# Block 1's positions in the order second half, first half, and T4 written over T2

## The chip, the cores and the metric

The kernel runs on one core of a Trainium2 chip. Five engines work side by side, each through its own queue in order: TensorE (PE, matrix products; PEld is its weight load), VectorE (DVE), ScalarE (ACT), GpSimd (POOL) and SyncE (SP, which issues transfers). The metric is the device time of one execution in microseconds; lower is better. The profile comes from one more execution, recorded by the hardware profiler.

## The reference

One encoder layer on x of 1024 positions by 1024 channels, float32: modulation, a Fourier mixing of positions and channels with a linear map, a layer norm, then a gated MLP with a convolution of width 3 over positions, and a last layer norm. The part that the change touches is the MLP's first product:

```python
def conv_gated_ffn(h, w_up, conv_w, conv_b, w_down):
    u = h @ w_up
    up = jnp.pad(u, ((0, 0), (1, 1), (0, 0)))
    u = up[:, :-2] * conv_w[0] + up[:, 1:-1] * conv_w[1] + up[:, 2:] * conv_w[2] + conv_b
    val, gate = u[..., :D_FF], u[..., D_FF:]
    return (jax.nn.gelu(gate, approximate=False) * val) @ w_down
```

D_FF is 2816, so w_up has 5632 columns.

## The kernel before

**Products.** Every float32 product is made of three TensorE products (hl3, L283 to L286): each operand is split into a high part, a float32r rounding made on ScalarE (L53), and a low part, the remainder, made on VectorE or GpSimd (L54); high by high, high by low and low by high are added in PSUM.

**Stages.** First comes the Fourier mixer, then the first norm, which leaves the modulated activations as eight tiles h2t0 to h2t7 (one for 128 channels, 1024 positions each, slots 0 to 7). Then the up-projection, in 22 blocks of 128 value columns and 128 gate columns (j = 0 to 21), and at the end the down-projection.

**Blocks 0 and 1** are multiplied plainly: for value and gate, 8 channel tiles times 3 products over the positions. Block 0 goes through four groups of positions as the activations become ready (their parts are Hh and Hl). Block 1 (L611 to L616) goes through the two halves of positions, ph, 512 each, and in each through v = 0 (value) and v = 1 (gate): four products of 24 matmuls. Its weights' parts, a1, lie in slots 33, 24, 25 and 26.

**Blocks 2 to 21** use Strassen's scheme: the activations are four quarters B (first or second half of channels, kh, by first or second half of positions, ph), and seven products of 12 matmuls replace eight. Four combinations of quarters are needed: T1 = B12 - B11, T2 = B22 - T1, T3 = B22 - B12, T4 = T2 - B21, where the second index is the half of positions. Their raw forms come from comb (L532): T1 and T3 in slots 34 and 35, T2 in 46 and 47, T4 in 31 and 32. t_op (L521) splits T1, T2, T4 into slots of their own; T4's parts go into slots 24, 44, 25 and 26, which hold parts of a0 and a1 until blocks 0 and 1 are multiplied. T3's parts overwrite B12's, that is Hh and Hl of the first four channel tiles, second half of positions (L617 to L619): blocks 2 to 21 don't need B12 itself.

**A block's weights.** Raw halves of block j are two tiles wu (512 KB each); for block 2 in slots 27 and 28, of which 28 first holds u0_0, the value part of block 0 before its convolution. GpSimd makes four sums: S1 and S2 in S12 (slot 31), S3 and S4 in S34 (slot 32); S1 and S4 need the second raw half, S3 only the first (L633 to L636). Seven operands a (A11, S2, S1, A12, S3, S4, A22: products 0 to 6) are split into slots 33, 34, 35, 45, 46, 47 and 48. A block ends in gated (L573): three passes of the convolution for value and gate (L578 on ScalarE, L579 and L580, the taps, on VectorE), GELU (L582), the product, and a write of the result to memory, issued by GpSimd (L588).

**What sets the order.** The program is written block after block, and a list scheduler with a timeline model reorders the instructions of each engine; in this part nothing is ordered by hand. A tile in a slot waits until the last reader of the slot's tile before has finished.

Of the kernel before, what the change touches and what calls it, by code (L numbers as in the profile page):

```python
# [8 lines left out]
F32 = mybir.dt.float32  # L9
F32R = mybir.dt.float32r  # L10
AF = mybir.ActivationFunctionType
ALU = mybir.AluOpType
# [12 lines left out]
ON_POOL = frozenset((  # L25
    "H0", "H1", "T1", "T2", "T4", "a0", "a1", "c1l0", "c1l1", "c1l2", "fb0_0", "fb0_512", "fb1_0", "fe00_512",
    "lb1_512", "lb2_512", "lb3_512", "le00_0", "le10_512", "s0_512", "s2_0", "s3_512", "ve2",
# [9 lines left out]
def encoder_layer(ctx: ExitStack, tc: tile.TileContext, I, out: bass.AP):  # L37
# [8 lines left out]
    def slot(i, shape, dt, name):  # L46
        return big.tile([128] + list(shape), dt, tag=f"s{i}", name=name)
# [4 lines left out]
    def split(hi, lo, src, eng=None):  # L52
        act.activation(hi, src, AF.Copy)  # L53
        (eng or dve).tensor_tensor(lo, src, hi, ALU.subtract)  # L54

    def E(name):
        return pool if name in ON_POOL else dve
# [42 lines left out]
    def xbank(name):  # L100
        n_x[0] += 1
        return bank(n_x[0] % 8, name)
# [326 lines left out]
    for n_t, t in enumerate((1, 2, 0, 3)):  # L429
        ts_ = slice(128 * t, 128 * t + 128)  # L430
        xr = []
        for m, src in ((0, I["x"]), (1, I["xm"])):
            v = slot(25 + (2 * n_t + m) % 3, [D], F32, f"xr{t}_{m}")
# [71 lines left out]
    B = {(kh, ph): [h2t[4 * kh + q][:, 512 * ph : 512 * ph + 512] for q in range(4)] for kh in range(2) for ph in range(2)}  # L505
# [15 lines left out]
    def t_op(name, n, pieces):  # L521
        hi, lo = [], []
        for i in range(2):
            h = slot(T_slots[16 + 4 * n + 2 * i], [2, 512], F32R, f"T{name}h{i}")
            l = slot(T_slots[17 + 4 * n + 2 * i], [2, 512], F32R, f"T{name}l{i}")
            for q in range(2):
                split(h[:, q, :], l[:, q, :], pieces[2 * i + q])
                hi.append(h[:, q, :])
                lo.append(l[:, q, :])
        ops[name] = (hi, lo)  # L530

    def comb(name, x, y, op, sl):  # L532
        out_ = []
        for i in range(2):
            v = slot(sl + i, [2, 512], F32, f"{name}_{i}")
            for q in range(2):
                E(name).tensor_tensor(v[:, q, :], x[2 * i + q], y[2 * i + q], op)
                out_.append(v[:, q, :])
        return out_

    cw = cp.tile([128, NB, 2, 4], F32, name="cw")
# [25 lines left out]
    def plain_mm(acc, w, v, g):  # L567
        for k in range(KT):
            hl3(acc, *w[k, v], g(Hh[k]), g(Hl[k]), k == 0, k == KT - 1)
# [3 lines left out]
    def gated(j, u_v, u_g):  # L573
        tv = []
        for v, u in ((0, u_v), (1, u_g)):
            tt = slot(3 + (2 * j + v) % 3, [S], F32, f"t{j}_{v}")
            w = cw[:, j, v, :]
            act.activation(tt, u, AF.Identity, scale=w[:, 1:2], bias=w[:, 3:4])  # L578
            dve.scalar_tensor_tensor(tt[:, 1:S], u[:, 0 : S - 1], w[:, 0:1], tt[:, 1:S], ALU.mult, ALU.add)  # L579
            dve.scalar_tensor_tensor(tt[:, 0 : S - 1], u[:, 1:S], w[:, 2:3], tt[:, 0 : S - 1], ALU.mult, ALU.add)  # L580
            tv.append(tt)
        act.activation(tv[1], tv[1], AF.Gelu)  # L582
        gg = u_g

        dve.scalar_tensor_tensor(gg[:, 0:512], tv[0][:, 0:512], -1.0, tv[1][:, 0:512], ALU.mult, ALU.mult)
        dve.tensor_tensor(gg[:, 512:513], tv[0][:, 512:513], tv[1][:, 512:513], ALU.mult)
        dve.tensor_tensor(gg[:, 513:1024][:, ::-1], tv[0][:, 513:1024], tv[1][:, 513:1024], ALU.mult)  # L587
        pool.dma_start(gd[j], gg)  # L588
# [3 lines left out]
    for gi, g in enumerate(GRP):  # L592
        for k in range(KT):
            split(g(Hh[k]), g(Hl[k]), g(h2t[k]), E(f"H{gi}") if k % 2 else dve)
        for v in range(2):
# [4 lines left out]
            for k in ((), (), (0, 1), (2, 3), (4, 5), (6, 7), (), ())[2 * gi + v]:  # L600
                ada_mm(G2, l_g2, bk=2, kts=(k,))
    a1 = plain_w(1, (33, 24, 25, 26))
    T1 = comb("T1", B[0, 1], B[0, 0], ALU.subtract, 34)
    T2 = comb("T2", B[1, 1], T1, ALU.subtract, 46)
    t_op("T2", 1, T2)
    t_op("T1", 0, T1)
    T3 = comb("T3", B[1, 1], B[0, 1], ALU.subtract, 34)
    T4 = comb("T4", T2, B[1, 0], ALU.subtract, 31)
    gated(0, u0[0], u0[1])
    u1 = [slot((2, 0)[v], [S], F32, f"u1_{v}") for v in range(2)]  # L610
    for ph in range(2):  # L611
        for v in range(2):
            g = slice(512 * ph, 512 * ph + 512)
            acc = xbank(f"x1_{ph}{v}")
            plain_mm(acc, a1, v, lambda a: a[:, g])
            act.activation(u1[v][:, g], acc, AF.Copy)  # L616
    ops["T3"] = ops["B12"]  # L617
    for q in range(4):
        split(ops["T3"][0][q], ops["T3"][1][q], T3[q])  # L619
    t_op("T4", 2, T4)  # L620
    gated(1, u1[0], u1[1])
# [3 lines left out]
    for j in range(2, NB):  # L625
# [12 lines left out]
        def product(n, a, tname):  # L638
            o = slot(A_slots[n], [2, 4, 128], F32R, f"a{j}_{n}")
            split(o[:, 0], o[:, 1], a)  # L640
            acc = xbank(f"x{j}_{n}")
            th, tl = ops[tname]
            for kt in range(4):
                hl3(acc, o[:, 0, kt, :], o[:, 1, kt, :], th[kt], tl[kt], kt == 0, kt == 3)
            return acc
# [9 lines left out]
        x = product(0, A11, "B11")  # L655
        act.activation(p1, x, AF.Copy)
        x = product(1, S2, "T2")
# [3 lines left out]
        x = product(3, A12, "B21")  # L661
        dve.tensor_tensor(uv_[:, 0:512], x, p1, ALU.add)
        x = product(4, S3, "T3")
        dve.tensor_tensor(u3, x, u2, ALU.add)
        dve.tensor_tensor(ug_[:, 512:], x5, u3, ALU.add)
        x = product(5, S4, "B22")
        dve.tensor_tensor(uv_[:, 512:], x, u4, ALU.add)
        x = product(6, A22, "T4")
        dve.tensor_tensor(ug_[:, 0:512], u3, x, ALU.subtract)
# [423 lines left out]
```

## Time and profile before

| | us |
|---|---|
| three runs | 865.58, 866.10, 866.92 |
| median | 866.1 |
| profiled execution | 866.72 |
| its span | 864.9 |
| granted TensorE clock, mean over the span | 0.974 |
| TensorE busy | 799.9 |
| VectorE busy | 708.3 |
| ScalarE busy | 387.3 |
| GpSimd busy | 328.9 |

The span runs from the first to the last instruction of the recorded execution. "Busy" is the union of an engine's instructions; matmuls are pipelined, and their ends are modelled. Times in the views are microseconds from the start of the span. A timeline row has start, length, engine, line, operation, output and inputs, form and count, and in brackets the engine's idle time before it with what ended that.

### The profile page before, as it was taken

The numbers are of one execution on the slowest core, as the hardware profiler recorded it, in microseconds if no ns is written. First come the engines' busy times: TensorE is split into PE (matmuls) and PEld (weight loads), VectorE is DVE, ScalarE is ACT, GpSimd is POOL, SyncE is SP. The second block draws the span as 40 slices with busy tenths as digits, with TensorE's granted clock in tenths as the row PEclk, the third lists the DMA queues.
The fourth block names the chain that finished last, engine by engine and source line by source line (L and its number), as shares of the span: only waits on it lengthen the run. The fifth ranks groups of instructions, "written<-read, shape, count | busy, mean of one in ns | idle before, by whom it ended". The sixth has DMA issues, their size and how long they took to land.

```text
span 864.9 us, 10742 instructions
## 1 busy us (share of the span) xinstructions
PE 799.9 (92%) x3943; PEld 644.2 (74%) x3943; DVE 708.3 (82%) x979; ACT 387.3 (45%) x559; POOL 328.9 (38%) x256
## 2 busy tenths in 40 slices
PE   2699799997979999999999999999999989999990
PEld 1466577776868888888888888888887868888880
DVE  6972857899899999998888888888677784556897
ACT  7442514676454344444444444444444324335611
POOL 5767802498355434334334333431000112702203
PEclk9899899999989999999999999999999999999995
DMA  9759665562113222322212222210498887988903
GB/s 342 260 181 309 248 230 210 186 262 74 49 49 97 98 74 74 111 84 98 74 73 74 87 90 92 98 50 25 156 375 309 264 215 147 190 157 240 294 26 122
DMA packets 50613, 133.90 MB, mean 155 GB/s; under 512 B 5608, under 2 KB 6760, under 8 KB 50560
## 3 DMA queue, kind: packets, MB, share of 16 engines
q1 hardware_dynamic: 39504, 103.59, 34.1%
q0 software_dynamic: 10768, 28.58, 13.4%
q10 hardware_dynamic: 288, 1.05, 0.3%
q8 instruction: 31, 0.51, 0.2%
q14 instruction: 22, 0.18, 0.1%
HBM read 110.39 MB, written 19.92 MB: 151 GB/s over the span
## 4 chain that ended last, share of the span: by engine, by line
PE 57%; DVE 6%; DMA 6%; issue 2%; POOL 1%; ACT 1%; SPq 0%; POOLq 0%; ACTq 0%; DVEq 0%
PE x L286 14%; PE x L284 14%; PE x L285 14%; PE o L285 5%; PE o L286 5%; PE o L284 5%; DMA gr<-gd 2%; DMA xu<-x1d 2%; DMA wd<-in_w_down_dram 1%; DVE d_1l L54 1%; DVE d_0l L54 1%; DMA Sg<-gd 1%; DVE C L864 1%; POOL S L635 0%; DVE C L894 0%
## 5 line engine op out<-in xcount | busy, mean ns | idle before, releaser
L285 PE MATMUL x<-Hl,a 128*128 128x512 f32 (+2 forms) x416 | 156.7, 378 | 4.8 <-DVE Hl L54 4.0
L284 PE MATMUL x<-Hh,a 128*128 128x512 f32 (+2 forms) x416 | 155.6, 377 | 4.6 <-ACT a L53 4.6
L286 PE MATMUL x<-Hh,a 128*128 128x512 f32 (+2 forms) x416 | 155.9, 375 | 0.0
L285 PE MATMUL o<-d_1l,d_0h 128*128 128x512 f32 (+1 forms) x299 | 115.0, 386 | 4.0 <-DVE d_1l L54 4.0
L286 PE MATMUL o<-d_1h,d_0l 128*128 128x512 f32 (+1 forms) x299 | 114.4, 384 | 0.0
L284 PE MATMUL o<-d_1h,d_0h 128*128 128x512 f32 (+1 forms) x299 | 102.8, 383 | 0.0
L285 PEld LDWEIGHTS x<-Hl,a 128*128 128x128 f32 x416 | 79.0, 190 | 20.2 <-DVE Hl L54 5.1
L284 PEld LDWEIGHTS x<-Hh,a 128*128 128x128 f32 x416 | 78.5, 190 | 20.8 <-ACT a L53 5.5
L53 ACT ACTIVATE a<-S 128x512 fp32r<-128x512 f32 x80 | 50.4, 630 | 96.2 <-PE x L286 87.9
L286 PEld LDWEIGHTS x<-Hh,a 128*128 128x128 f32 x416 | 79.0, 190 | 14.6 <-POOL nbm L478 0.4
L588 POOL DMA_DIRECT2D gd<-ug x20 | 11.4, 568 | 170.2 <-DVE ug L587 170.2
L285 PEld LDWEIGHTS o<-d_1l,d_0h 128*128 128x128 f32 x299 | 56.8, 190 | 16.5 <-DVE d_1l L54 5.3
L54 DVE TENSOR_TENSOR a<-wu,a 128x512 fp32r<-128x512 f32 x60 | 63.5, 1059 | 3.0 <-ACT a L53 3.0
L286 PEld LDWEIGHTS o<-d_1h,d_0l 128*128 128x128 f32 x299 | 56.6, 189 | 10.9
L284 PEld LDWEIGHTS o<-d_1h,d_0h 128*128 128x128 f32 x299 | 56.2, 188 | 11.0
L54 DVE TENSOR_TENSOR a<-S,a 128x512 fp32r<-128x512 f32 x80 | 60.9, 762 | 0.8
L635 POOL TENSOR_TENSOR S<-wu 128x512 f32<-128x512 f32 x20 | 29.9, 1493 | 69.1 <-DVE a L54 60.4
L53 ACT ACTIVATE a<-wu 128x512 fp32r<-128x512 f32 x60 | 37.5, 626 | 40.5 <-PE x L286 38.6
L733 POOL DMA_DIRECT2D Sg<-gd x12 | 14.7, 1266 | 89.3 <-DVE d_0l L54 89.3
L579 DVE SCALAR_TENSOR_TENSOR t<-uv,cw,t 128x1023 f32<-128x1023 f32 x20 | 35.9, 1793 | 11.4 <-ACT t L578 11.3
L54 DVE TENSOR_TENSOR d_1l<-wd,d_1h 128x1024 fp32r<-128x1024 f32 (+1 forms) x37 | 44.0, 1189 | 0.0
L636 POOL TENSOR_TENSOR S<-wu,S 128x512 f32<-128x512 f32 x20 | 43.9, 2195 | 0.1
(325 smaller groups left out, 1929.7 us busy)
## 6 DMA issues: line engine op xcount, KB each, us to landing
aw<-in_ada_w_dram SPq DMA_DIRECT2D x48, 512.0 KB, 6.0
wu<-in_w_up_dram SPq DMA_DIRECT2D x44, 512.0 KB, 3.2
gd<-ug POOLq DMA_DIRECT2D x20, 512.0 KB, 2.9
wd<-in_w_down_dram SPq DMA_DIRECT2D x20, 512.0 KB, 9.7
gr<-gd SPq DMA_DIRECT2D x15, 512.0 KB, 7.4
gA<-gd SPq DMA_DIRECT2D x10, 512.0 KB, 10.7
Sg<-gd POOLq DMA_DIRECT2D x10, 512.0 KB, 6.5
x<-in_x_dram SPq DMA_DIRECT2D x8, 512.0 KB, 5.4
```

The lines of the kernel that those rows point to most:

```text
L53: act.activation(hi, src, AF.Copy)
L54: (eng or dve).tensor_tensor(lo, src, hi, ALU.subtract)
L284: pe.matmul(ps_ap, hi_l, hi_r, start=first, stop=False)
L285: pe.matmul(ps_ap, hi_l, lo_r, start=False, stop=False)
L286: pe.matmul(ps_ap, lo_l, hi_r, start=False, stop=last)
L579: dve.scalar_tensor_tensor(tt[:, 1:S], u[:, 0 : S - 1], w[:, 0:1], tt[:, 1:S], ALU.mult, ALU.add)
L588: pool.dma_start(gd[j], gg)
L635: pool.tensor_tensor(S3, A11, A21, ALU.subtract)
L636: pool.tensor_tensor(S4, A12, S2, ALU.subtract)
L733: pool.dma_start(raw_g[p, i] if p == 7 else Sg[i], gd[k0 : k0 + n, :, 512 * mh : 512 * mh + 512].rearrange("k p c -> p k c"), accum_op=ALU ...
L864: dve.scalar_tensor_tensor(c1[:, lo], c1[:, lo], rs, ffb[:, lo], ALU.mult, ALU.add)
```

## The change

Two edits. Block 1 takes the second half of positions first. And comb, when no slot is given, writes its result over its first operand; it is used so for T4, which now lies over T2's raw form in slots 46 and 47, and leaves slots 31 and 32 unused between block 0's weights and block 2's sums.

```diff
     def comb(name, x, y, op, sl):
         out_ = []
         for i in range(2):
-            v = slot(sl + i, [2, 512], F32, f"{name}_{i}")
+            v = slot(sl + i, [2, 512], F32, f"{name}_{i}") if sl is not None else None
             for q in range(2):
-                E(name).tensor_tensor(v[:, q, :], x[2 * i + q], y[2 * i + q], op)
-                out_.append(v[:, q, :])
+                o = x[2 * i + q] if v is None else v[:, q, :]
+                E(name).tensor_tensor(o, x[2 * i + q], y[2 * i + q], op)
+                out_.append(o)
         return out_
...
     T3 = comb("T3", B[1, 1], B[0, 1], ALU.subtract, 34)
-    T4 = comb("T4", T2, B[1, 0], ALU.subtract, 31)
+    T4 = comb("T4", T2, B[1, 0], ALU.subtract, None)
     gated(0, u0[0], u0[1])
     u1 = [slot((2, 0)[v], [S], F32, f"u1_{v}") for v in range(2)]
-    for ph in range(2):
+    for ph in (1, 0):
         for v in range(2):
```

The scheduler answers with another order around the start of block 2; from block 6 on, all queues are as before. In the rows below a tile's name ends in a running number; line numbers behind L533 are one higher in the change. TT4 are T4's parts, t0 and t1 the convolution tiles of blocks 0 and 1, u0 and u1 their inputs (_0 value, _1 gate), a2_n the split operand of block 2's product n, x2_n its result.

GpSimd's queue, from T2's last piece to block 2's sums, before:

```order
L537 TENSOR_TENSOR T2_1_2152<-h2t7_1116,T1_1_2146 128x512
L537 TENSOR_TENSOR T4_0_2185<-T2_0_2149,h2t4_1113 128x512
L537 TENSOR_TENSOR T4_0_2185<-T2_0_2149,h2t5_1114 128x512
L537 TENSOR_TENSOR T4_1_2188<-T2_1_2152,h2t6_1115 128x512
L537 TENSOR_TENSOR T4_1_2188<-T2_1_2152,h2t7_1116 128x512
L588 DMA gd_67<-u0_1_1824 128x1024
L635 TENSOR_TENSOR S34_2_2348<-wu2_0_2343 128x512
L633 TENSOR_TENSOR S12_2_2347<-wu2_0_2343,wu2_1_2345 128x512
L634 TENSOR_TENSOR S12_2_2347<-S12_2_2347,wu2_0_2343 128x512
```

GpSimd's queue at the same place in the change:

```order
L538 TENSOR_TENSOR T2_1_2152<-h2t7_1116,T1_1_2146 128x512
L538 TENSOR_TENSOR T2_0_2149<-T2_0_2149,h2t4_1113 128x512
L636 TENSOR_TENSOR S34_2_2346<-wu2_0_2341 128x512
L538 TENSOR_TENSOR T2_0_2149<-T2_0_2149,h2t5_1114 128x512
L538 TENSOR_TENSOR T2_1_2152<-T2_1_2152,h2t6_1115 128x512
L538 TENSOR_TENSOR T2_1_2152<-T2_1_2152,h2t7_1116 128x512
L634 TENSOR_TENSOR S12_2_2345<-wu2_0_2341,wu2_1_2343 128x512
L589 DMA gd_67<-u0_1_1824 128x1024
L635 TENSOR_TENSOR S12_2_2345<-S12_2_2345,wu2_0_2341 128x512
```

S3 (into S34) has moved between T4's pieces, and S1 ahead of the write of block 0's result.

VectorE's queue, around the taps of block 0 and T3's remainders (Hl), before:

```order
L579 SCALAR_TENSOR_TENSOR t0_1_2195<-u0_1_1824,cw_1801,t0_1_2195 128x1023
L579 SCALAR_TENSOR_TENSOR t0_0_2191<-u0_0_1823,cw_1801,t0_0_2191 128x1023
L580 SCALAR_TENSOR_TENSOR t0_1_2195<-u0_1_1824,cw_1801,t0_1_2195 128x1023
L580 SCALAR_TENSOR_TENSOR t0_0_2191<-u0_0_1823,cw_1801,t0_0_2191 128x1023
L585 SCALAR_TENSOR_TENSOR u0_1_1824<-t0_0_2191,t0_1_2195 128x512
L586 TENSOR_TENSOR u0_1_1824<-t0_0_2191,t0_1_2195 128x1
L587 TENSOR_TENSOR u0_1_1824<-t0_0_2191,t0_1_2195 128x511
L54 TENSOR_TENSOR a2_0_2357<-wu2_0_2343,a2_0_2357 128x512
L54 TENSOR_TENSOR a2_3_2408<-wu2_1_2345,a2_3_2408 128x512
L54 TENSOR_TENSOR a2_6_2460<-wu2_1_2345,a2_6_2460 128x512
L54 TENSOR_TENSOR Hl0_1793<-T3_0_2179,Hh0_1785 128x512
```

VectorE's queue at the same place in the change:

```order
L580 SCALAR_TENSOR_TENSOR t0_1_2193<-u0_1_1824,cw_1801,t0_1_2193 128x1023
L580 SCALAR_TENSOR_TENSOR t0_0_2189<-u0_0_1823,cw_1801,t0_0_2189 128x1023
L581 SCALAR_TENSOR_TENSOR t0_1_2193<-u0_1_1824,cw_1801,t0_1_2193 128x1023
L54 TENSOR_TENSOR Hl0_1793<-T3_0_2179,Hh0_1785 128x512
L581 SCALAR_TENSOR_TENSOR t0_0_2189<-u0_0_1823,cw_1801,t0_0_2189 128x1023
L54 TENSOR_TENSOR Hl1_1794<-T3_0_2179,Hh1_1786 128x512
L54 TENSOR_TENSOR Hl2_1795<-T3_1_2182,Hh2_1787 128x512
L54 TENSOR_TENSOR Hl3_1796<-T3_1_2182,Hh3_1788 128x512
L586 SCALAR_TENSOR_TENSOR u0_1_1824<-t0_0_2189,t0_1_2193 128x512
```

T3's four remainders have moved up; the first stands ahead of the last read of u0_0.

ScalarE's queue, where block 2's sums are split, before:

```order
L53 ACTIVATE TT4h0_2318<-T4_0_2185 128x512 x2
L616 ACTIVATE u1_1_2205<-x1_11_2284 128x512
L578 ACTIVATE t1_1_2334<-u1_1_2205,cw_1801 128x1024
L656 ACTIVATE p12_2_2353<-x2_0_2360 128x512
L53 ACTIVATE a3_0_2504<-wu3_0_2490 128x512
L53 ACTIVATE a2_4_2425<-S34_2_2348 128x512
L53 ACTIVATE a3_3_2555<-wu3_1_2492 128x512
L53 ACTIVATE a2_2_2391<-S12_2_2347 128x512
L53 ACTIVATE a2_1_2374<-S12_2_2347 128x512
```

ScalarE's queue at the split of the same sums in the change:

```order
L53 ACTIVATE a2_0_2355<-wu2_0_2341 128x512
L53 ACTIVATE a2_3_2406<-wu2_1_2343 128x512
L53 ACTIVATE a2_2_2389<-S12_2_2345 128x512
L617 ACTIVATE u1_0_2202<-x1_00_2256 128x512
L53 ACTIVATE TT4h1_2322<-T2_1_2152 128x512 x2
L579 ACTIVATE t1_0_2328<-u1_0_2202,cw_1801 128x1024
L53 ACTIVATE a2_1_2372<-S12_2_2345 128x512
L53 ACTIVATE TT4h0_2316<-T2_0_2149 128x512 x2
L53 ACTIVATE a2_6_2458<-wu2_1_2343 128x512
```

The splits of S1 (a2_2) and S2 (a2_1) have moved ahead of half of T4's. TensorE follows: before, it ran block 2's products 0 and 3, one matmul of 6, two of block 3's product 0, two of 4 and then the rest of 6; now it runs product 0, one matmul of 2, two of 1, four of 2, the rest of 1 and of 2, and then 3, 4, 5, 6, each whole.

## Rows read from the trace of the kernel before

**Rows 1.** The page, part 1: engine, busy us, share of the span, instructions.

```profile
PE 799.9 (92%) x3943; PEld 644.2 (74%) x3943; DVE 708.3 (82%) x979; ACT 387.3 (45%) x559; POOL 328.9 (38%) x256
```

**Rows 2.** Waits of TensorE, 230 to 300 us: total us, times, longest.

```profile
PE x L284 <- ACT a L53: 4.6, 2, 2.5
```

**Rows 3.** Windows of 60 us: busy us (instructions) by engine, granted clock, DMA.

```profile
300.00:360.00 60.00, 60.00 (x267) 49.69 (x266) 57.14 (x71) 25.71 (x36) 25.78 (x20) 1.00 0.24 88
```

**Rows 4.** Timeline of TensorE, start of block 2.

```profile
237.58 0.39 PE L284 MATMUL x<-Hh,a 128*128 128x512 f32 x1
...
243.02 0.39 PE L284 MATMUL x<-TT4h,a 128*128 128x512 f32 x1
245.56 0.50 PE L284 MATMUL x<-Hh,a 128*128 128x512 f32 x1 [2.15 <-ACT a L53]
...
248.78 0.80 PE L284 MATMUL x<-Hh,a 128*128 128x512 f32 x1 [2.48 <-ACT a L53]
...
253.88 0.39 PE L286 MATMUL x<-Hh,a 128*128 128x512 f32 x1
```

**Rows 5.** Windows of 2 us, columns as in rows 3.

```profile
248.00:250.00 2.00, 1.22 (x3) 1.03 (x4) 2.00 (x2) 1.15 (x2) 2.00 (x2) 0.50 0.00 0
```

**Rows 6.** Timeline of ScalarE, splits of blocks 1 and 2.

```profile
234.89 0.63 ACT L53 ACTIVATE a<-wu 128x512 fp32r<-128x512 f32 x1 [1.07 <-DMA wu<-in_w_up_dram]
...
238.40 0.62 ACT L53 ACTIVATE Hh<-T 128x512 fp32r<-128x512 f32 x1
238.92 1.23 ACT L578 ACTIVATE t<-u,cw 128x1024 f32<-128x1024 f32 x1
...
248.10 0.63 ACT L53 ACTIVATE a<-S 128x512 fp32r<-128x512 f32 x1 [2.59 <-POOL S L635]
```

**Rows 7.** Timeline of GpSimd, block 0's write and block 2's sums.

```profile
234.76 0.63 POOL L588 DMA_DIRECT2D gd<-u  x1 [9.72 <-DVE u L587]
244.09 3.97 POOL L635 TENSOR_TENSOR S<-wu 128x512 f32<-128x512 f32 x1 [8.70 <-ACT u L616]
248.03 2.25 POOL L633 TENSOR_TENSOR S<-wu,wu 128x512 f32<-128x512 f32 x1
250.36 1.61 POOL L634 TENSOR_TENSOR S<-S,wu 128x512 f32<-128x512 f32 x1
```

**Rows 8.** Timeline of VectorE, taps of block 0 and splits of T4.

```profile
229.11 2.46 DVE L580 SCALAR_TENSOR_TENSOR t<-u,cw,t 128x1023 f32<-128x1023 f32 x2
...
238.53 0.69 DVE L54 TENSOR_TENSOR a<-wu,a 128x512 fp32r<-128x512 f32 x1 [2.28 <-ACT a L53]
...
242.66 1.29 DVE L54 TENSOR_TENSOR TT4l<-T,TT4h 128x512 fp32r<-128x512 f32 x2
...
245.66 1.28 DVE L54 TENSOR_TENSOR TT4l<-T,TT4h 128x512 fp32r<-128x512 f32 x2
```

**Rows 9.** Instructions on T, 200 to 260 us: ns min/median/max, first and last start.

```profile
L537 POOL TENSOR_TENSOR T<-h2t x4: 1309/1394/1492, 201.2 to 208.3; 128x512 f32<-128x512 f32 x4
...
L54 DVE TENSOR_TENSOR TT2l<-T,TT2h x4: 677/1222/1778, 217.5 to 226.1; 128x512 fp32r<-128x512 f32 x4
```

**Rows 10.** The page, part 6: transfers, median us to landing.

```profile
wu<-in_w_up_dram SPq DMA_DIRECT2D x44, 512.0 KB, 3.2
```

**Rows 11.** Waits of SyncE's queue, 600 to 720 us, columns as in rows 2.

```profile
SPq L687 <- PE x L286: 40.7, 1, 40.7
...
SPq L797 <- DMA xu<-x1d: 14.2, 1, 14.2
```

**Rows 12.** Timeline of TensorE, two earlier waits.

```profile
196.11 0.39 PE L285 MATMUL x<-Hl,a 128*128 128x256 f32 x1 [1.07 <-DVE Hl L54]
...
211.83 0.39 PE L285 MATMUL x<-Hl,a 128*128 128x258 f32 x1 [1.79 <-DVE Hl L54]
```

**Rows 13.** Windows of 10 us, columns as in rows 3.

```profile
190.00:200.00 10.00, 8.04 (x71) 6.01 (x69) 9.07 (x27) 6.29 (x18) 8.39 (x9) 1.00 0.30 107
...
210.00:220.00 10.00, 8.21 (x48) 7.71 (x48) 10.00 (x12) 4.73 (x12) 7.61 (x6) 0.83 0.10 37
```

## The prediction, made before the change was run

> **What bounds the kernel now.** The page's busy shares come first: TensorE works 799.9 of 864.9 us [rows 1], so only its idle or slow stretches can be won back. The waits list of TensorE from 230 to 300 us has one line, ScalarE's splits (L53), 4.6 us in two waits [rows 2]. In 300:360 us TensorE is busy 60.00 of 60 us, as in the four windows of 60 us behind it (the first of the five is shown) [rows 3], and the up-projection has no other hole after block 2 begins. The timeline shows the hole: a matmul at 243.02, two from 245.56 on, the next at 248.78 us [rows 4]. That is block 2's start. The 0.227 us pitch is (243.02 - 237.58) / 24, the 24 matmuls between those two rows. [...]
>
> Why it waits: the split at 248.10 was released by GpSimd's L635, S3, which began at 244.09 after 8.70 us of idleness and took 3.97 us [rows 6, 7]. GpSimd then ran S1 (248.03) and S2 (250.36). The slot of S3, 32, held T4 until VectorE had split T4: the splits that begin at 242.66 free T4's second half, and 244.09 follows their end, 242.66 + 1.29 = 243.95 [rows 8]. (The row names ScalarE's copy, L616, as releaser; S3 waits for both engines, and VectorE is the later.) T4's split in turn sat behind T3's on both engines, and T3's could not start before the second half of block 1's positions was multiplied. So two buffer reuses, not arithmetic, make the hole.
>
> **The change part by part.** No instruction is added or removed. TensorE's four products of block 1 keep their length (24 matmuls each), and block 2's first product still begins at about 237.6 us. Nothing changes before 218 us.
>
> (a) Positions in the order 1, 0. T3 overwrites Hh and Hl of the second half; its readers now finish with v=1's first twelve matmuls, some 11 us earlier (two products of 24 x 0.227 = 5.44). T3's four splits, on ScalarE and VectorE, move ahead of the GELU of block 0, to a time just before one in which VectorE idled, 2.28 us in its longest wait [rows 8]. The slots of T3's raw form, which block 2's S2 and S1 splits need, come free with them. Price: on VectorE one of these splits (Hl0, 0.6 us from start to start) stands ahead of the last read of u0_0, whose slot takes block 2's raw half 1.
>
> (b) T4 over T2. T4 no longer waits for block 0's products on slots 31 and 32, and S12, S34 no longer wait for T4. S3 runs on GpSimd about 220 us, behind the first piece of T4. T4's four pieces now each wait for T2's split; the last of these begins at 226.1 us [rows 9] and takes 0.7. So one T4 piece runs beside block 0's taps (L579, L580). What such a meeting costs VectorE is in its T2 splits, most of which ran beside T4's pieces: 677 ns shortest, 1778 longest [rows 9]. I take +1.1 us, the difference; the low end is 0, because that piece may fall between two VectorE instructions.
>
> (c) The new path to block 2's second product. Before, u0_0's last read ends at 229.11 + 2.46 = 231.57 [rows 8]. Now 231.57 + 1.1 + 0.6 = 233.3. The 512 KB load behind it needs 3.3 us (before: 231.57 to 234.89, where the split that it released begins; the page's median is 3.2) [rows 6, 10]: 236.6. S1 on GpSimd needs it. S1 took 2.25, S2 1.61, S3 3.97, all beside VectorE [rows 7]; VectorE then has only short gating pieces left, so I take 1.7 for S1, near S2's, ending at 238.3, and keep 1.3 and 3.97 as ends (1.3 from GpSimd's shortest T piece, 1309 ns [rows 9]). ScalarE then has a2_2, the copy u1_0, two T4 splits, block 1's first pass (L578) and only then a2_1: five of about 0.6 us and one of 1.23 [rows 6], less 0.1 for each because the next starts before the last has ended (238.40 to 238.92 for one of 0.62): 238.3 + 5 x 0.6 + 1.23 - 5 x 0.1 = 242.0, and with the hand-overs between engines 242.3 us. GpSimd reaches S2's end earlier, 238.3 + 0.6 (the gd write ahead of it [rows 7]) + 1.6 = 240.5, so ScalarE's queue decides.
>
> TensorE ends x2_0 at 237.58 + 12 x 0.227 = 240.3, does one matmul of x2_2 until 240.5, and waits for a2_1: **1.8 us**. Then VectorE's a2_1 remainder, behind block 1's first tap (241.7 + 1.2) and its own 0.68, is there at 243.6 to 244.7, and TensorE asks at 242.3 + 6 x 0.227 = 243.7: I take **0.3**. Last, a2_4's remainder: VectorE has four T4 splits (1.28 for two [rows 8]), a tap, a2_6, a tap and itself to do after a2_1, 4 x 0.6 + 1.2 + 0.6 + 1.2 + 0.7 = 6.1 us, from 244.0 to 250.1, or 252.3 if two GpSimd sums meet it at 1.1 each. TensorE asks at 237.58 + 50 x 0.227 + 2.1 = 251.0: between 0 and 1.3, I take **0.5**. After that T4's last use and the raw operands of block 3 have microseconds in hand: x2_6 comes seventh now.
>
> Sum: 7.2 - 1.8 - 0.3 - 0.5 = **4.6 us won**, with the clock granted in full. What follows passes it on: TensorE is the bound from 254 to 612 us, and the first loads of the down-projection wait for its last matmul (40.7 us in one wait on SyncE's queue [rows 11]), so that stage moves as a whole. The profiled execution took 866.72 us, its span 864.9 with 1.8 around it, and 866.1 is the median: the span should fall to 860.3, the time to 866.1 - 4.6 = 861.5 us. About 0.2%, 1.7 us, is what a measurement of this kernel can tell from no change.
>
> [...]
>
> **The rivals.**
>
> *The clock falls once more.* The stretch 240.5 to 244 us still holds 1.8 + 0.3 us of idleness. Before, waits of 1.07 us left the granted clock at 1.00 in 190:200, but one of 1.79 us at 211.83 came with 0.83 in 210:220 [rows 12, 13]. Mine lies on the larger side. The price by the rows: 2.6 us after the old hole; a granted clock of 0.83 over 10 us is 1.7 us of full-rate work lost. I take 2.1; the fall would swallow the 0.5 us wait for a2_4, so 1.6 more is lost: 4.6 - 1.6 = 3.0 won, 863.1 us. [...]
>
> *The hole closes wholly.* If T4's last piece misses VectorE (-1.1) and S1 takes 1.3 (-0.4), a2_1 is there at 240.8 and everything else follows in time: 7.2 - 0.3 = 6.9 won, 859.2 us. Against it: two of T2's four splits took over 1222 ns, against 677 for the shortest [rows 9].
>
> *No change: the down-projection gives it back.* SyncE's queue has a wait of 14.2 us on a transfer there [rows 11]. If those were paced by memory from a fixed time, up to 4.6 us would go: 866.1. Against it: the chain of those loads begins with the wait for TensorE's last up matmul.
>
> *Slower: GpSimd is starved.* If VectorE held it off in S1 and S2 as it did in S3, 3.97 us each, S2 would end at 236.6 + 3.97 + 0.6 + 3.97 = 245.1 and a2_1 be split at 245.8: a wait of 5.3 us, the old hole under another name, with its 2.6 us of low clock and a late a2_4 (0.5). That loses 8.4, 1.2 more than before: 867.3. It decides against the change from S1 + S2 of about 6.8 us on (7.2 - 2.6 - 0.5 leaves a wait of 4.1); before, the same two took 2.25 + 1.61 = 3.9, with VectorE more crowded than it will be.
>
> *The change does not do what it says* if the earlier T3 splits do not run earlier. Their queue places did move, so this is part of the starved case.
>
> **How the numbers follow.** Forecast 861.5 us: 0.47, its own range 860.5 to 862.5. Clock falls, 863.1: 0.28. Hole closes, 859.2: 0.11. Given back, 866: 0.08. Starved, 867.3: 0.06. The range that leaves out two in ten at most reaches from 858.9 (the whole 7.2 won) to 864.7 (1.4 won: S1 at 3.97 instead of 1.7, and the a2_4 wait at its upper end, 1.3). Faster by over 1.7 us: the first three, 0.86; within 0.2%: 0.08; slower: 0.06.
>
> **What would show it.** In the profile after: GpSimd's S3 near 220 us, in between T4's pieces; the last read of u0_0 at 233 us and the split that its load releases at 236.6; TensorE waiting once near 240.5 us for a split, for about 2 us, and no 2.5 us gap near 246; the first matmul of block 3's second product at about 262 us (before, the same count of matmuls was reached at 253.88 + 56 x 0.227 = 266.6); the later stages shifted by the same amount. Granted clock 1.00 from 238 to 256 us speaks for the forecast, below that for the first rival. It would be wrong if a different wait, of VectorE on its longer backlog say, showed after 262 us, or if the shift at 262 us were not found at the end.

## The result: 0.50% faster

The change takes 862.4 us (median of 11 runs) against 866.2 us for the kernel before, run beside it; the ratio is 0.9950, 95% interval 0.9936 to 0.9964. It is not the ratio of the two medians, which lie 3.8 us or 0.44% apart. Ratios here and below are of fast executions alone; one of e7's twelve, at 1624 us, is not among them. The profiled execution took 862.41 us with a span of 860.6 (before 864.9). Forecast were 861.5 us and a span of 860.3. The page of the change, part 1 (engine, busy us, share, instructions):

```profile
PE 798.8 (93%) x3943; PEld 643.7 (75%) x3943; DVE 704.8 (82%) x979; ACT 387.0 (45%) x559; POOL 327.8 (38%) x256
```

The instruction counts are those of [rows 1]. TensorE's waits from 230 to 300 us in the change (total us, times, longest), the answer to [rows 2], where ScalarE's splits cost 4.6 us in two waits:

```profile
PE x L286 <- DVE a L54: 0.8, 1, 0.8
```

The hole is closed to one wait for a VectorE remainder. TensorE's timeline in the change, against [rows 4] (start, length, engine, line, operation, output and inputs, form, count, idle before):

```profile
239.80 0.39 PE L284 MATMUL x<-Hh,a 128*128 128x512 f32 x1
...
242.52 0.39 PE L284 MATMUL x<-TT1h,a 128*128 128x512 f32 x1
242.93 0.50 PE L284 MATMUL x<-TT2h,a 128*128 128x512 f32 x1
...
251.33 0.39 PE L285 MATMUL x<-Hl,a 128*128 128x512 f32 x1
252.55 0.50 PE L286 MATMUL x<-Hh,a 128*128 128x512 f32 x1 [0.84 <-DVE a L54]
...
263.14 0.39 PE L284 MATMUL x<-TT2h,a 128*128 128x512 f32 x1
```

One measure serves all that follows: **the 96 matmuls** from block 2's first on, start of the first to start of the 97th. They take 266.60 - 237.58 = 29.02 us before, 263.14 - 239.80 = 23.34 in the change, and 96 x 0.227 = 21.8 without a hole, at the step of 0.227 us from matmul to matmul in [rows 4]. So 5.7 us were won here. But block 2 began 2.2 us later than in [rows 4], so only 3.5 us remained at the 97th matmul, as at the last one of the up-projection, and 4.3 at the last one of all; where the other 0.8 us came from is open.

That lateness lies ahead of the change's first effect. Windows of 10 us in the change (busy us and instructions of PE, PEld, DVE, ACT, POOL, then granted clock, DMA share, GB/s):

```profile
210.00:220.00 10.00, 8.22 (x40) 7.54 (x40) 10.00 (x12) 3.46 (x9) 7.76 (x6) 0.66 0.13 52
...
240.00:250.00 10.00, 9.98 (x44) 7.76 (x43) 9.12 (x8) 7.24 (x13) 6.38 (x4) 1.00 0.27 105
```

With instructions in the same order there and the same two waits for Hl, 0.89 and 1.78 us (before: 1.79 in [rows 12] and the 0.88 below), the granted clock from 210 to 220 us was 0.66 instead of 0.83 [rows 13]; another 1.0 us of lateness was there from 182 us on (a matmul at 182.03 that began at 181.00 before). The row of before:

```profile
208.72 0.39 PE L285 MATMUL x<-Hl,a 128*128 128x258 f32 x1 [0.88 <-DVE Hl L54]
```

Block 2 itself ran at a granted clock of 1.00 in the change, in every window of 2 us from 236 to 258. The other engines in the change, ScalarE, GpSimd and VectorE, the counterparts of [rows 6 to 8]:

```profile
237.56 0.64 ACT L53 ACTIVATE a<-wu 128x512 fp32r<-128x512 f32 x1 [1.71 <-DMA wu<-in_w_up_dram]
...
242.26 0.61 ACT L53 ACTIVATE a<-S 128x512 fp32r<-128x512 f32 x1
```

```profile
221.18 1.45 POOL L636 TENSOR_TENSOR S<-wu 128x512 f32<-128x512 f32 x1 [0.26 <-PE x L286]
...
237.60 1.43 POOL L634 TENSOR_TENSOR S<-wu,wu 128x512 f32<-128x512 f32 x1 [7.47 <-DMA wu<-in_w_up_dram]
```

```profile
227.70 3.50 DVE L580 SCALAR_TENSOR_TENSOR t<-u,cw,t 128x1023 f32<-128x1023 f32 x2
...
232.93 1.27 DVE L581 SCALAR_TENSOR_TENSOR t<-u,cw,t 128x1023 f32<-128x1023 f32 x1
```

S3 runs at 221 us, between T4's pieces, instead of 244; the last read of u0_0 ends at 234.20; the load that it releases ends 3.36 us later, at 237.56; S1 follows; a2_1 is split at 242.26. Behind block 2 nothing gives the gain back: SyncE's queue still has its wait of 40.7 us for TensorE, and the one of [rows 11] for a transfer (L797 there) is 14.3 us:

```profile
SPq L688 <- PE x L286: 40.7, 1, 40.7
...
SPq L798 <- DMA xu<-x1d: 14.3, 1, 14.3
```

### The profile page after: what moved, and what is told of

Its sections match the earlier page's. It is cut to its first block, busy times and chain, and to the rows that moved or that the text cites. A ratio compares the mean times of both kernels' runs of the same rounds, so it can differ in the third digit from the quotient of the medians.

```text
span 860.6 us, 10737 instructions
## 1 busy us (share of the span) xinstructions
PE 798.8 (93%) x3943; PEld 643.7 (75%) x3943; DVE 704.8 (82%) x979; ACT 387.0 (45%) x559; POOL 327.8 (38%) x256
## 4 chain that ended last, share of the span: by engine, by line
PE 75%; DVE 15%; DMA 4%; issue 2%; POOL 2%; ACT 1%; POOLq 0%; SPq 0%; ACTq 0%; DVEq 0%
PE x L286 15%; PE x L285 15%; PE x L284 15%; PE o L285 6%; PE o L286 6%; PE o L284 6%; PE ada L136 2%; DMA xu<-x1d 2%; PE B L285 1%; PE B L286 1%; DVE fe L198 1%; DVE Hl L54 1%; PE B L284 1%; PE A L285 1%; PE A L284 1%
## 5 line engine op out<-in xcount | busy, mean ns | idle before, releaser
L54 DVE TENSOR_TENSOR a<-wu,a 128x512 fp32r<-128x512 f32 x60 | 60.9, 1015 | 0.3 <-ACT a L53 0.3
L636 POOL TENSOR_TENSOR S<-wu 128x512 f32<-128x512 f32 x20 | 26.9, 1347 | 68.4 <-DVE a L54 68.2
```

Source lines behind the costliest of these rows:

```text
L636: pool.tensor_tensor(S3, A11, A21, ALU.subtract)
```

## The experiments

Each ratio is to runs of the kernel before on the same chip, with its 95% interval; the other columns come from one profiled execution each, and two of one kernel differ there: block 2 began at 239.80 us in the change and at 237.12 in after_again.

| kernel | ratio | block 2's first matmul | the 96 matmuls | 97th matmul |
|---|---|---|---|---|
| before | 1 | 237.58 | 29.02 | 266.60 |
| change | 0.9950 (0.9936 to 0.9964) | 239.80 | 23.34 | 263.14 |
| after_again | 0.9946 (0.9926 to 0.9966) | 237.12 | 25.26 | 262.38 |
| e1_order_only | 0.9961 (0.9946 to 0.9975) | 238.78 | 25.57 | 264.35 |
| e2_t4_only | 0.9986 (0.9972 to 0.9999) | 238.31 | 27.93 | 266.24 |
| e3_wu2_slot1 | 0.9973 (0.9959 to 0.9987) | 240.49 | 25.43 | 265.92 |
| e4_hl_first | 0.9932 (0.9917 to 0.9946) | 236.35 | 26.09 | 262.44 |
| e6_t4_dve | 0.9917 (0.9899 to 0.9936) | 239.89 | 22.09 | 261.98 |
| e7_hl_first_t4_dve | 0.9965 (0.9951 to 0.9978) | 234.77 | 29.86 | 264.63 |
| e9_hl_first_t24_dve | 0.9918 (0.9895 to 0.9940) | 232.75 | 27.11 | 259.86 |
| e10_e9_slot1 | 0.9928 (0.9912 to 0.9945) | 234.70 | 27.19 | 261.89 |
| e11_e10_s2dve | 0.9862 (0.9840 to 0.9885) | 235.37 | 21.82 | 257.19 |

**The change once more (after_again).** No edit.

> The change itself once more, beside the other kernels on one chip. Theory: in the first profiled execution of the change block 2's first matmul began 2.2 us late, at 239.8 us, because the clock fell for longer at 212 us, and this lateness covered the wait for a2_1 that the prediction had counted. If it begins at about 237.6 us here, the 96 matmuls from it on take 24 to 25 us (21.8 + 1.8 + 0.3 + 0.5 = 24.4), with a visible wait for ScalarE's a2_1; if it begins near 239.8 us again, 23.3 us. The end time is the same in both cases, 0.9936 to 0.9964 of the kernel before. Rival: 23.3 us whatever the start; the predicted wait was simply not there.

Block 2 began at 237.12 us, and the wait was there. TensorE's waits from 236 to 275 us, its timeline, and the window around it:

```profile
PE x L284 <- ACT a L53: 2.0, 1, 2.0
PE x L286 <- DVE a L54: 0.8, 1, 0.8
```

```profile
237.12 0.39 PE L284 MATMUL x<-Hh,a 128*128 128x512 f32 x1
...
239.84 0.39 PE L284 MATMUL x<-TT1h,a 128*128 128x512 f32 x1
242.20 0.50 PE L284 MATMUL x<-TT2h,a 128*128 128x512 f32 x1 [1.97 <-ACT a L53]
...
251.78 0.50 PE L286 MATMUL x<-Hh,a 128*128 128x512 f32 x1 [0.83 <-DVE a L54]
...
262.38 0.39 PE L284 MATMUL x<-TT2h,a 128*128 128x512 f32 x1
```

```profile
240.00:250.00 10.00, 8.03 (x35) 6.34 (x35) 9.12 (x10) 7.28 (x12) 5.60 (x4) 1.00 0.21 82
```

One matmul of x2_2, then 1.97 us for a2_1, as predicted. The 25.26 us are a little above the expected 24 to 25. The rival, that the wait was not there, falls: in the first execution a2_1's split came at 242.26 and TensorE asked for it only at about 242.7, so lateness had covered nearly all of it. The two ratios, 0.9950 and 0.9946, agree.

**One edit at a time (e1, e2).** e1 takes block 1 in the order 1, 0 and leaves T4 in slots 31 and 32; e2 is the reverse.

```diff
-    for ph in range(2):
+    for ph in (1, 0):
```

> Only the first edit: block 1's positions in the order 1, 0; T4's raw form stays in slots 31 and 32. Measure: the 96 matmuls from block 2's first on, 29.0 us before, 23.3 in the change, 96 x 0.227 = 21.8 without a hole. My theory says that both reuses bound the hole. T3's splits are out of the way, so T4's splits on VectorE end near 245.5 instead of 246.9 us, but GpSimd's S1, S3, S2 still wait for them: its first sum starts at 244 to 246 us, TensorE waits once for 1.5 to 3 us after x2_0, x2_3, x2_6, and the 96 matmuls take 24 to 27 us: 2 to 5 us won, about 863 us. Rival 'the order alone does it': 23.3 us, and the time of the change, 0.995 of the kernel before. Rival 'the order is worth nothing without the slots': 28.5 to 29.5 us, ratio 0.998 to 1.001.

```diff
-    T4 = comb("T4", T2, B[1, 0], ALU.subtract, 31)
+    T4 = comb("T4", T2, B[1, 0], ALU.subtract, None)
```

> Only the second edit: T4 over T2; block 1's positions in the old order 0, 1. GpSimd's S3, S1, S2, S4 run before 241 us. My theory: T3's splits now free the slots of a2_1 and a2_2 too late: ScalarE reaches a2_1 at 241 to 243 us and a2_2 and a2_4 only after VectorE has split T3 and T4. The 96 matmuls from block 2's first take 24 to 27 us (before 29.0, change 23.3, without a hole 21.8), with waits of TensorE for VectorE's remainders rather than for GpSimd's sums: about 863 us. Rival 'the slots alone do it': 23.3 us and a ratio of 0.995. Rival 'nothing without the order': 28.5 to 29.5 us and a ratio within 0.2% of 1.

e1's sums behave as its theory said: GpSimd's first still waits for T4's splits, and comes at 245.17 us, no earlier than before (244.09).

```profile
245.17 2.20 POOL L633 TENSOR_TENSOR S<-wu,wu 128x512 f32<-128x512 f32 x1 [6.83 <-DVE TT4l L54]
```

25.57 us lie in the expected 24 to 27, but not by the one wait of 1.5 to 3 us that was expected: TensorE ran products 0, 3 and 6 whole (36 matmuls, to 247.0 us) while the sums were being made, and then waited four times, 0.46, 1.37, 0.27 and 0.41 us, three of them for a VectorE remainder. e2 missed: 27.93 us, above my 24 to 27 and near the rival "nothing without the order". GpSimd's sums were done by 241.4 us, but ScalarE's a2_1 stood behind four T3 splits and two T4 splits, and came at 244.70; here the granted clock fell too (0.84 in 240 to 250). ScalarE and TensorE in e2:

```profile
243.18 1.14 ACT L53 ACTIVATE TT4h<-T 128x512 fp32r<-128x512 f32 x2
244.22 0.57 ACT L617 ACTIVATE u<-x 128x512 f32<-128x512 f32 x1
244.70 0.62 ACT L53 ACTIVATE a<-S 128x512 fp32r<-128x512 f32 x1
```

```profile
245.37 0.50 PE L284 MATMUL x<-TT2h,a 128*128 128x512 f32 x1 [1.02 <-ACT a L53]
```

By the ratios alone the order is worth 0.39% and the slots 0.14%, together 0.50 to 0.54%. What the slots are worth is not clear of noise: e2's interval ends at 0.9999, and e1's overlaps the change's, so the rival "the order alone does it" is not excluded by the times. The 96 matmuls do not exclude it either (25.57 in e1, 25.26 in after_again). The rows show only that in e1 the sums still waited for T4 and in the change they did not.

**The load out of the way (e3).** The change, with block 2's second raw half in a slot that is free earlier.

```diff
-        sl = (24, 27) if j == 0 else ((29, 30) if j % 2 else (27, 28))
+        sl = (24, 27) if j == 0 else ((29, 30) if j % 2 else (27, 1 if j == 2 else 28))
```

> The change, and block 2's second raw half loaded into slot 1, which is free earlier, instead of slot 28, which waits for the last read of u0_0. It takes away the whole path of step (c): last read of u0_0, load, S1, S2, ScalarE's queue to a2_1. My theory: the load lands several us before 236.6 us, S1 and S2 are through before block 2 begins, and a2_1 is split before TensorE asks. What is left of the 1.6 us that the change still loses in its 96 matmuls is the wait for a2_4's remainder, which hangs on VectorE's backlog and not on this load: 22.0 to 23.0 us (change 23.3), time 0.3 to 1.3 us below the change. Rival 'nothing hangs on the load any more': 23.3 us and the time of the change. Rival 'the sums then meet VectorE's taps of block 0': those taps, and with them block 2's start, come 1 us or more later than 239.8 us, and the gain is gone.

The third case came, in part: slower than the change (0.9973; the intervals just overlap), though still faster than before. Block 2's start was 0.7 us behind 239.8, not 1 or more, and 3.4 us behind after_again's. GpSimd's S1, S2 and S4 moved to 227 to 236 us, into VectorE's taps, and lengthened them; VectorE in e3:

```profile
229.36 3.51 DVE L580 SCALAR_TENSOR_TENSOR t<-u,cw,t 128x1023 f32<-128x1023 f32 x2
232.80 2.30 DVE L581 SCALAR_TENSOR_TENSOR t<-u,cw,t 128x1023 f32<-128x1023 f32 x1
235.02 1.78 DVE L54 TENSOR_TENSOR a<-wu,a 128x512 fp32r<-128x512 f32 x1
```

A tap alone takes 1.27 us, such a remainder 0.68. T3's remainders and block 2's first operands then came late, and TensorE waited at the start of block 2 instead:

```profile
240.49 0.50 PE L284 MATMUL x<-Hh,a 128*128 128x512 f32 x1 [1.92 <-ACT a L53]
...
242.93 0.79 PE L286 MATMUL x<-Hh,a 128*128 128x512 f32 x1 [1.71 <-DVE a L54]
```

This suggested a new theory, which the runs below try: behind both reuses the bound is VectorE's backlog from 204 to 256 us, and GpSimd's sums lengthen it.

**The last activations first (e4).** The change, with VectorE's remainders of the last group's Hl ahead of those of T1 and T2.

```diff
+            last_h = split(g(Hh[k]), g(Hl[k]), g(h2t[k]), E(f"H{gi}") if k % 2 else dve)
...
+    with tc.issue_after(last_h.ins):
+        t_op("T2", 1, T2)
+        t_op("T1", 0, T1)
```

> The change, and VectorE's remainders of the last group of activations (Hl) ahead of those of T1 and T2. In before, TensorE waits 0.88 and 1.79 us for an Hl behind which the clock falls; in the profiled execution of the change the clock stayed low about twice as long there, and block 2's first matmul began at 239.8 instead of 237.6 us. Theory: the remainders of T1 that stand in between cause both waits; without them the granted clock stays at 1.00 from 206 to 220 us, block 2's first matmul begins 3 to 5 us before 239.8 us, at 235 to 237, and since VectorE's total work is the same, part of it comes back as longer 96 matmuls, 23.5 to 25.5 us: time 1 to 4 us below the change. Rival 'the Hl are late for another reason, the norm ahead of them': waits of 0.9 and 1.8 us stay, start at 237.6 to 239.8 us, the time of the change. Rival 'all given back': the start comes earlier by 3 us or more and the 96 matmuls grow by as much, the time of the change.

Half right: from 210 to 220 us the granted clock was 1.00, with one wait of 0.8 us left, and block 2 began at 236.35. But the 96 matmuls grew to 26.09 us, above the expected range: a wait ahead of the first (1.01), and two behind it, the longer for a VectorE remainder at 242.09 (1.08), with a granted clock of 0.83 in 240 to 250. Against the change, the intervals of 0.9932 and 0.9950 overlap, and the 97th matmul came no earlier than in after_again: most was given back. That this is because VectorE's work was only put in another order is my reading; no run tests it.

**T4's pieces on VectorE (e6).** The change, with one name out of the set of GpSimd's operations.

```diff
-    "H0", "H1", "T1", "T2", "T4", "a0", "a1", "c1l0", "c1l1", "c1l2", "fb0_0", "fb0_512", "fb1_0", "fe00_512",
+    "H0", "H1", "T1", "T2", "a0", "a1", "c1l0", "c1l1", "c1l2", "fb0_0", "fb0_512", "fb1_0", "fe00_512",
```

> The change, and T4's four pieces on VectorE instead of GpSimd. In the change's trace every GpSimd piece that falls into VectorE's busy stretch from 204 to 256 us makes one VectorE instruction with two inputs 1.1 us longer (1.78 for 0.68); VectorE itself needs 0.6 us for such a piece. Theory: 4 x (1.1 - 0.6) = 2 us of VectorE's time come free before the last read of u0_0 (232.9 us in the change), so that read, the load behind it and GpSimd's S1 come 1 to 2.5 us earlier and the stall on a2_1 is gone whenever block 2 starts; the time is 0.3 to 2 us below the change's, the 96 matmuls from block 2's first on take 22 to 23.5 us. Rival 'VectorE has more to do': it is 2.4 us later there, block 2's splits come late, the 96 matmuls take over 24 us, slower than the change.

The stretch came as expected, 22.09 us without a wait of TensorE from 232 to 275 us, and the time a little lower (0.9917, its interval touching the change's), although VectorE does more. But the way was not the expected one: the last read of u0_0 ended 4.4 us ahead of block 2's first matmul (5.6 in the change), so the load came no earlier; the scheduler now began product 3, which needs no sum, second. So e6 does not show what T4's pieces on VectorE are worth by themselves.

**e7 and e9** put e4's order and VectorE's pieces together: e7 with T4, e9 with T2 and T4 on VectorE.

> e4_hl_first, and T4's four pieces on VectorE. With the remainders of the last group first, block 2 began at 236.35 us, but 1.6 us of waits for ScalarE's splits and 1.1 for a VectorE remainder came up behind it, with a granted clock of 0.87 and 0.70 from 240 to 248 us: the 96 matmuls took 26.1 us. Theory: VectorE's backlog, lengthened by 1.1 us at each meeting with GpSimd, causes those waits; 2 us less of it leaves a start at 235.5 to 236.8 and 96 matmuls in 23 to 25 us: 1 to 3 us below e4_hl_first, about 0.990 to 0.992 of the kernel before. Rival 'the waits come from ScalarE's order or the load, not from VectorE': 26 us again, the time of e4_hl_first.

> e7_hl_first_t4_dve, and T2's four pieces on VectorE too. They ran on GpSimd from 210.8 to 217.0 us and met VectorE's remainders of T1 and of the activations. Theory by the same price: another 4 x (1.1 - 0.6) = 2 us of VectorE's time come free; but three of the pieces stand in VectorE's queue ahead of remainders that TensorE waits for, so at most half of that shows: block 2's start 235 to 237 us, 96 matmuls 22.5 to 24.5 us, time within -1.5 and +0.5 us of e7_hl_first_t4_dve. Rival 'the meetings cost GpSimd, not VectorE': 2.4 us more work on VectorE, start 237 us or later, slower than e7_hl_first_t4_dve by 1 us or more.

e7 missed badly: 0.9965 and 29.86 us. Its block 2 began at 234.77 us, but S3's operand a2_4 has slot 46, which since the second edit holds T4's raw form, and now came early in TensorE's order. ScalarE and TensorE in e7:

```profile
242.96 0.63 ACT L53 ACTIVATE a<-S 128x512 fp32r<-128x512 f32 x1 [3.16 <-DVE TT4l L54]
```

```profile
243.65 0.80 PE L284 MATMUL x<-Hh,a 128*128 128x512 f32 x1 [3.05 <-ACT a L53]
```

That is the price of T4 over T2, which the change's order of products hides. e9 began block 2 at 232.75 us, earlier than I expected, and its 96 matmuls took 27.11 us, longer than expected; at 0.9918 it was far below e7, not within 1.5 us of it.

**e10 and e11** take the load away from e9, and then the sums from GpSimd as well.

> e9_hl_first_t24_dve, and block 2's second raw half in slot 1 as in e3_wu2_slot1. In e9_hl_first_t24_dve block 2 began at 232.75 us, but the raw half landed only at 235.7 us, GpSimd's S1 began then, and the 96 matmuls took 27.1 us. Theory: there the load behind the last read of u0_0 is the bound, as step (c) of the prediction had it; with slot 1 S1 and S2 run before 232 us, three of GpSimd's sums meet VectorE at 1.1 us each, so block 2 starts 0 to 3 us later, at 232.7 to 236 us, and the 96 matmuls take 22 to 25 us: 0 to 3 us below e9_hl_first_t24_dve, ratio 0.988 to 0.992. Rival, as in e3_wu2_slot1: the sums' meetings with VectorE cost as much as the load, block 2's operands come late, the ratio stays at 0.992 or gets worse.

```diff
-        pool.tensor_tensor(S1, A21, A22, ALU.add)
+        es = dve if j == 2 else pool
+        es.tensor_tensor(S1, A21, A22, ALU.add)
```

(and S2, S3, S4 alike)

> e10_e9_slot1, and block 2's four sums S1 to S4 on VectorE instead of GpSimd: 4 x 0.6 = 2.4 us of VectorE's time, against 1.1 us at each meeting. Theory: GpSimd has nothing in VectorE's stretch from 212 to 236 us any more, all of VectorE's two-input instructions there last 0.68 or 1.28 us, and against e10_e9_slot1 up to 4 x (1.1 - 0.6) = 2 us are saved: time within -2 and +0.5 us of it. Rival 'few of the sums met VectorE': 2.4 us more work on VectorE, 1 to 2.4 us slower than e10_e9_slot1.

e10 was e3's case again: the load was early, S1, S2 and S4 ran from 228 to 235 us, two taps took 2.31 us each, one T3 remainder 1.77, and nothing was won over e9 (0.9928; the intervals overlap). VectorE in e10:

```profile
229.50 2.31 DVE L581 SCALAR_TENSOR_TENSOR t<-u,cw,t 128x1023 f32<-128x1023 f32 x1
231.74 2.31 DVE L580 SCALAR_TENSOR_TENSOR t<-u,cw,t 128x1023 f32<-128x1023 f32 x1
233.97 1.77 DVE L54 TENSOR_TENSOR Hl<-T,Hh 128x512 fp32r<-128x512 f32 x1
```

But e10 does not test the load alone. e9's three waits behind its start (1.60, 0.59 and 1.49 us, from 237 to 244) were gone, block 2 began 2 us later, and one new wait came, 2.6 us ahead of the matmul at 250.17, with a granted clock of 0.81 from 248 to 252 and 0.77 from 252 to 256. It comes from one more reuse: slot 48, which a2_6 needs, holds u0_1 until block 0's result, made in its place, is written. That write stood in GpSimd's queue behind block 3's S2, which took 4.10 us beside VectorE. TensorE's wait, ScalarE and GpSimd in e10:

```profile
PE x L284 <- ACT a L53: 2.6, 1, 2.6
```

```profile
249.48 0.63 ACT L53 ACTIVATE a<-wu 128x512 fp32r<-128x512 f32 x1 [3.18 <-DMA gd<-u]
```

```profile
242.38 4.10 POOL L636 TENSOR_TENSOR S<-S,wu 128x512 f32<-128x512 f32 x1
246.43 0.63 POOL L589 DMA_DIRECT2D gd<-u  x1
```

So whether the load bounds e9 stays open. e11 won more than expected, 5.7 us over e10 instead of 2 at most: **0.9862, 855.2 us**, some 1.4% below the kernel before. VectorE in e11 by shape, 212 to 246 us (busy us, mean ns), then windows with TensorE never idle:

```profile
L581 DVE SCALAR_TENSOR_TENSOR t<-u,cw,t 128x1023 f32<-128x1023 f32 x3 | 3.8, 1271 | 0.0
L580 DVE SCALAR_TENSOR_TENSOR t<-u,cw,t 128x1023 f32<-128x1023 f32 x3 | 3.8, 1271 | 0.0
...
L538 DVE TENSOR_TENSOR T<-h2t,h2t 128x512 f32<-128x512 f32 x4 | 2.6, 683 | 0.0
```

```profile
212.00:236.00 24.00, 24.00 (x124) 20.58 (x123) 23.65 (x38) 15.78 (x27) 0.22 (x1) 1.00 0.12 43
...
240.00:264.00 24.00, 24.00 (x108) 19.81 (x107) 24.00 (x31) 10.78 (x16) 16.83 (x10) 1.00 0.19 71
```

The same view of after_again, 212 to 246 us:

```profile
L538 DVE TENSOR_TENSOR T<-h2t,h2t 128x512 f32<-128x512 f32 x4 | 5.9, 1502 | 0.0
L581 DVE SCALAR_TENSOR_TENSOR t<-u,cw,t 128x1023 f32<-128x1023 f32 x3 | 4.9, 1619 | 0.0
L580 DVE SCALAR_TENSOR_TENSOR t<-u,cw,t 128x1023 f32<-128x1023 f32 x3 | 4.8, 1641 | 0.9 <-ACT t L579 0.9
```

The same ten T3 pieces and taps cost 5.9 + 4.9 + 4.8 = 15.6 us there and 10.2 in e11. Against e10, one edit away: there each of block 2's four sums lengthened one VectorE instruction (S3 a remainder at 218.78 us, 1.78 for 0.68; the others those shown above), 4.3 us in all. In e11 none of VectorE's two-input instructions from 217 to 246 us is lengthened, and the sums cost it 4 x 0.6 = 2.4. With GpSimd out of this stretch the 96 matmuls take 21.82 us, all that the pitch asks for. But two things went at once, the lengthening and the wait for block 0's write, which e11 issues at 242.54, ahead of block 3's sums. How the 5.7 us divide between them is not tested.

## Why the prediction was right

- **The hole and its two causes**: the first is borne out: with T3's splits earlier, e1 alone is 0.39% faster. Of the second the rows show the mechanism (S3 at 221 us instead of 244, no wait for T4's slots), but its worth is not told apart from nothing (above). The hole was not nearly closed in both executions: of the 7.2 us, after_again won back 3.8 and the first execution 5.7, the more because its block 2 began late.
- **Path (c)**, against after_again, whose block 2 began near the assumed 237.6 us. The wait for a2_1, predicted 1.8, was 1.97 us; its split came at 241.53 us (242.3 predicted, 242.26 in the first execution). The terms ahead of it: T4's last piece lengthened a tap (3.51 us for the first two; a pair alone takes 2.46 [rows 8], so +1.0 for +1.1 predicted), the load took 3.4 (3.3), S1 1.45 (1.7, between the bounds 1.3 and 3.97). GpSimd's S1 and ScalarE's split of a2_1 in after_again:

```profile
236.86 1.45 POOL L634 TENSOR_TENSOR S<-wu,wu 128x512 f32<-128x512 f32 x1 [7.46 <-DMA wu<-in_w_up_dram]
```

```profile
241.53 0.62 ACT L53 ACTIVATE a<-S 128x512 fp32r<-128x512 f32 x1
```

- **a2_1's remainder**: 0.3 predicted, no wait seen.
- **a2_4's remainder**: 0.5 predicted, 0.83 us idle, and 1.2 from start to start instead of 0.23, so 1.0 lost. Undersized, inside its bounds 0 to 1.3; by the rows the cause is the named one, VectorE's backlog met by block 3's first sums (a tap of 2.31 us for 1.27 at 244.1).
- **Sum**: 7.2 - 1.8 - 0.3 - 0.5 = 4.6 us predicted. The 7.2 is in [rows 4]: from 243.02 to 253.88 us 16 matmuls take 10.86 us and need 16 x 0.227 = 3.63; 2.15 + 2.48 of the difference are idle, and the other 2.6, the price that the rivals use, are slower steps, with a granted clock of 0.50 in 248 to 250 [rows 5]. Measured 0.50 and 0.54% of 866 to 867 us, 4.3 and 4.7, with intervals from 2.9 to 6.4; in after_again the last matmul came 844.03 - 839.58 = 4.45 us earlier than before. That it fits so closely is in part luck. The 96 matmuls of after_again lost 25.26 - 21.8 = 3.5 us and not the predicted 2.6: from start to start the two waits cost 2.1 and 1.0, and slower steps, most of them just behind the waits, 0.4. So this stretch won 29.02 - 25.26 = 3.8 us, and most of the rest is that block 2 happened to begin 0.5 us earlier than before. The range's upper end is off by 0.1 us in itself: with S1 at 3.97 instead of 1.7 the wait for a2_1 is 1.8 + 2.3 = 4.1, and 7.2 - 4.1 - 0.3 - 1.3 leaves 1.5 us won, 864.6.
- **Passed on**: the gain of 4.2 us at after_again's 97th matmul is the same 4.2 at the up-projection's last matmul and 4.45 at the end. "Given back" falls.
- **The clock**: it stayed at 1.00 in block 2 of the change, in after_again even behind a wait of 1.97 us. The rival with chance 0.28 did not come, but it could have: in e2, e3, e4, e7 and e10 the granted clock fell behind the waits of that stretch (0.82 to 0.84 over 10 us in e2, e3 and e4; over 4 us down to 0.50 in e7 and 0.77 in e10), while in e9, with waits of 1.60 and 1.49 us, it stayed at 1.00. These runs do not say what makes the difference, so that it stayed is in part luck.
- **GpSimd starved**: not here. S1 and S2 took 1.45 and 1.31 us in after_again; VectorE had idle moments of 0.33, 0.15 and 0.88 us around them. In denser stretches sums took longer (4.10 us in e10, 4.61 in e11).

What the prediction did not see: the first profiled execution hid the wait for a2_1 behind an unrelated lateness. Read alone, it would have said that the term of 1.8 us was wrong.

## What to carry to other kernels

When a stall is put down to the reuse of a buffer, look also at who fills the time between release and use: here, behind two reuses stood a VectorE backlog that GpSimd's sums lengthened, and freeing a third buffer (e3, e10) moved those sums into it; in e10 another reuse then set the wait. Where VectorE was dense, a two-input sum given to GpSimd lengthened a VectorE instruction by up to 1.1 us, while VectorE did such a sum itself in 0.6. Before a term of a predicted sum is called wrong, see whether the step ahead of it began when the sum assumed; and before a sum is called right, add up its terms from the trace.

## What the runs showed of the hardware

**A GpSimd sum cost VectorE more than the sum.** From 204 to 256 us I counted GpSimd's two-input elementwise instructions (over 1 us, nearly all 128x512) and VectorE's two-input instructions that took over 0.95 us (elementwise) or 1.5 us (taps): 15 and 15 before, 19 and 18 in the change, 20 and 19 in after_again, 17 and 17 in e1, 18 and 16 in e2, 20 and 20 in e3, 19 and 17 in e4, 16 and 15 in e6, 16 and 14 in e7, 11 and 11 in e9, 13 and 13 in e10, 10 and 8 in e11. Each of VectorE's is longer by up to 1.1 us (1.78 for 0.68, 2.31 for 1.27), while VectorE does such a sum in 0.6 us from start to start (e11: 229.24 to 229.84). The two counts never lie more than two apart.

**A GpSimd sum lasted through several VectorE instructions.** In e11, GpSimd's first sum of block 3 while VectorE ran without a pause:

```profile
243.34 4.61 POOL L636 TENSOR_TENSOR S<-wu,wu 128x512 f32<-128x512 f32 x1 [0.17 <-DVE a L54]
```

VectorE began five instructions in that time, the last of them, at 246.73 us, itself lengthened (2.30 us); GpSimd's shortest such sums took 1.3 us (1.29 in the kernel before). S3 in [rows 7] with 3.97 us was of this kind, and S3 in e6 and e9, with 6.49 and 8.26 us, more so. What sets the length of such a sum is left open by these runs.

**The clock answered alike waits differently.** Waits of 0.9 and 1.8 us ahead of 213 us came with a granted clock of 0.83 from 210 to 220 us before and 0.66 in the change. e1, with waits of 1.78 and 0.95 us that lay further apart (ahead of 212.63 and 217.19) and TensorE busy only 6.84 of these 10 us, kept 1.00:

```profile
210.00:220.00 10.00, 6.84 (x47) 5.82 (x46) 10.00 (x10) 4.95 (x12) 8.65 (x7) 1.00 0.16 52
```

What decides it stays open.
